# Attention scores and a recurrent gate as alternating 64-row products in place of stacked 128-row products

## The chip, the core and the metric

The kernel runs on one core of one Trainium2 chip. The metric is the device time of one execution in microseconds (us); smaller is better. The core has a matrix engine (TensorE, in the profile PE, and PEld for its loading of weights), VectorE (DVE), ScalarE (ACT), GpSimd (POOL) and SyncE (SP), which issues the transfers.

## What is computed

One decoder layer on 512 tokens of 1024 features. The parts that the change touches, cut from the reference:

```
qa = rms_norm(qa...); ka = rms_norm(ka...)                 # 8 heads of 64 features
s = einsum('bnqkgd,bnskd->bnkgqs', qb, kb) * HEAD_DIM**-0.5    # sliding window: own and previous block of 128 keys
...
s_own = einsum('bqhd,bshd->bqhs', q_c, k_c) * scale + own_bias # second attention (MoBA): 8 heads of 64 features
...
r = sigmoid(einsum('bsnc,ncd->bsnd', xb, ga_w) + ga_b)     # recurrence: 16 blocks of 64 features, two gates each
i = sigmoid(einsum('bsnc,ncd->bsnd', xb, gx_w) + gx_b)
```

Everything else (the input projection, the value products, the merge, the output projection, the gated MLP) is the same in both kernels.

## The kernel before

Features lie on the 128 partitions and tokens along the free axis. Every float32 operand of a product is split into a high part h with the 12 leading bits and a low part l (`split`), both in the type that TensorE takes at one column per cycle; a product x·y is made of the three passes h·h, h·l and l·h (`mm3`).

Scores and gates have a contraction of 64 features, half of the array's 128 rows. The kernel before fills the other half by stacking. A head of q (`turn_task`, key "q") has its high part on its own 64 partitions and its low part on the other 64; a head of k (key "k") has its high part on both halves of one tile and its low part on both halves of another, with two transfers per head that copy one half to the other. Then two passes of 128 rows make one head: stacked q against high k gives qh·kh + ql·kh, stacked q against low k gives qh·kl + ql·kl. `head_task` issues for each of the four query blocks of a head such a pair, over the keys that this block sees: 256, 256, 256 and 128 columns in a sliding-window head (kind "swa"), 512, 384, 256 and 128 in the other attention (kind "moba"). `lru_task` does the same for a recurrent gate: two blocks of 64 features, each stacked (high on one half, low on the other), two passes of 512 columns for each block, 8 times.

What follows a head's scores: VectorE adds the bias and takes the maximum (`E.ttr`), ScalarE takes exponentials, the matrix is transposed on TensorE (`E.tr`), split and multiplied with the values.

The order of the instructions is not written by hand. Every operation goes through the class `Emitter`, which records it; `flush` then simulates the engines with rough costs and lets each engine take the first operation whose operands are there. TensorE's long rows of work are the projections (`project`, and the loops over `qk` and `vc`), in the order of the table `ORDER`; the steps of attention and recurrence are generators that yield what they need (`Need`: tiles, PSUM banks, buffers) and are taken up between the products of the projections (`pump`). `FLY` says how many heads are in flight.

Of the kernel before, what the change touches and what calls it, by code (L numbers as in the profile page):

```python
# [25 lines left out]
# Columns of the per-feature vectors ("vec" input): feature f of a vector sits at partition f % 128,  # L26
# column f // 128 of its range.
# [8 lines left out]
# Columns of the shape-only constants ("cst" input).  # L36
# [24 lines left out]
class Buf:  # L61
    """A tile that is used again and again; Tile orders its uses, the emitter picks the ones that are free."""
# [21 lines left out]
class Emitter:  # L84
    """Emits instructions engine by engine and keeps a rough clock of each engine, so that the tensor engine's
    stream takes up work of the side tasks when its operands are there. The order it picks is one of many right
    ones: Tile puts in every wait."""
# [92 lines left out]
    # instructions  # L180
    def mm(self, out, lhsT, rhs, start, stop):
# [3 lines left out]
        else:  # L185
            cost = 4 * max(n, 128) / 2400 if n > 2 else 0.02
        self._go("pe", cost, [out], [lhsT, rhs], lambda: self.nc.tensor.matmul(out, lhsT, rhs, start=start, stop=stop),  # L187
                 rows=lhsT.shape[0] / 128)

# [78 lines left out]
    # the order of issue  # L268
    def flush(self):
        """Issue what was recorded: every engine takes, of its next few instructions, the first whose operands are  # L270
        there, by the same rough clock. Instructions that touch the same buffer keep their order."""
# [26 lines left out]
        def pe_cost(t, i):  # L298
            """The tensor engine runs at half its clock in a window that follows one with little work."""
# [54 lines left out]
    def cast(self, out, in_):  # L354
        """Copy (rounding to out's type) on whichever of the two engines would be done first."""
# [7 lines left out]
    def scale(self, out, in_, col):  # L363
        """out = in_ * col on whichever of the two engines would be done first."""
# [7 lines left out]
    def split(self, hi, lo, x):  # L372
        """hi + lo = x exactly, hi with the 12 leading bits."""
# [7 lines left out]
    def mm3(self, out, wh, wl, xh, xl, first, last):  # L381
        """out (+)= w.T x in three passes; what is left out is the product of the two low parts, below 2^-24."""
# [4 lines left out]
    # side tasks  # L387
# [34 lines left out]
    def pump(self, limit=LIMIT, force=False):  # L422
        """Take up steps of the side tasks that are ready, the oldest first, up to about limit us of tensor work."""
# [45 lines left out]
def hybrid_trunk_kernel(ctx: ExitStack, tc: tile.TileContext, xT, vec, cvec, cst, chot, rel, wm, w8, wz, wgate, wbr,  # L469
# [88 lines left out]
    def rsqrt(out, ssq, n, inv):  # L558
        """out = (ssq * inv + eps) ** -0.5: a first guess from the exponent, then three Newton steps."""
# [10 lines left out]
    def token_ssq(bk, sq, c0, nb, first=True, last=True):  # L570
        """Sums of squares over the features, a token per partition, a block of tokens per column."""
# [4 lines left out]
    def rsqrt_sqrt(out, st, ssq, n):  # L576
        """out = (ssq / D + eps) ** -0.5 from its rough square root st, by one Newton step."""
# [40 lines left out]
    # c on every partition; the sums of squares of x, a token per partition, beside it  # L618
# [12 lines left out]
    def warm(n):  # L631
        """Work for the tensor engine while it waits, so that its clock is up when the projections start."""
# [141 lines left out]
    def norm_task(bs, out, copy=False, v_first=None):  # L774
        """The banks bs with 8 heads each -> out, normalised but for the gain."""
# [27 lines left out]
    def turn_task(tn, srcs, gain, env, key):  # L803
        """Four blocks [token, feature] of two heads -> [feature, token], times the gain, split. A head of q has its
        high part on one half of the partitions and its low part on the other; a head of k has each part on both."""
        yield Need(tasks=(tn,))
        src = srcs()
        yield Need(aps=[x for x in src], banks=1, rslots=4 if key == "k" else 2)
# [3 lines left out]
        if key == "q":  # L812
            env["q"] = [E.rslot(), E.rslot()]
        else:
            env["kh"], env["kl"] = [E.rslot(), E.rslot()], [E.rslot(), E.rslot()]
        for u in range(2):
            p, o = half(u), half(1 - u)
            g, z = gain[p], bk.ap[p]
            if key == "q":
# [3 lines left out]
            else:  # L823
# [11 lines left out]
    def take_v(env, src, its):  # L835
        """src [token, (block, u, d)] of the token blocks its -> per block and head the high and the low parts."""
# [17 lines left out]
    def head_task(kind, tasks, qenv, kenv, venv, u, hd, oenv):  # L854
# [3 lines left out]
        if swa:  # L858
            loc = {3: (0, 0, 256), 2: (0, 256, 256), 1: (1, 0, 256), 0: (1, 256, 128)}
            keys = {i: max(i - 1, 0) * 128 for i in range(4)}  # L860
            ploc = {0: (0, 0, (0, 1)), 1: (0, 256, (1, 2)), 2: (1, 0, (2, 3)), 3: (1, 256, (3,))}
        else:
            loc = {3: (0, 0, 512), 2: (1, 0, 384), 0: (1, 384, 128), 1: (2, 0, 256)}
            keys = {i: 0 for i in range(4)}
            ploc = {0: (0, 0, (0, 1, 2, 3)), 1: (1, 0, (1, 2, 3)), 3: (1, 384, (3,)), 2: (2, 0, (2, 3))}
        wid = 256 if swa else 512
        sink = v("sinks", hd) if swa else -3.0e38
        yield Need(tasks=tasks, slots=nb + 1)
        T = E.slot()
        bias_tile(T.ap[:, :wid], d_swa if swa else d_moba, hd, wid)  # L870
        yield Need(aps=(qenv["q"][u].ap, kenv["kh"][u].ap, kenv["kl"][u].ap, T.ap), banks=nb,
                   slots=nb)
        bks = [E.bank() for _ in range(nb)]
        pr = [E.slot() for _ in range(nb)]
        mx, ngm, sm, ri = small(4), small(4), small(4), small(4)
        q, kh, kl = qenv["q"][u].r, kenv["kh"][u].r, kenv["kl"][u].r
        for i in (3, 2, 1, 0):
            b, c, n = loc[i]
            qs, ks = slice(i * 128, i * 128 + 128), slice(keys[i], keys[i] + n)
            E.mm(bks[b].ap[:, c:c + n], q[:, qs], kh[:, ks], True, False)  # L880
            E.mm(bks[b].ap[:, c:c + n], q[:, qs], kl[:, ks], False, True)
        for i in (3, 2, 1, 0):
            b, c, n = loc[i]
            E.ttr(pr[b].ap[:, c:c + n], bks[b].ap[:, c:c + n], T.ap[:, :n][:, ::-1], sink, OP.add,
                  OP.max, mx[:, i:i + 1])
# [609 lines left out]
```

## Time and profile before

| | |
|---|---|
| time, median of 3 runs | 907.24 us (906.32 to 908.49) |
| profiled execution, first to last instruction (span) | 904.7 us |
| PE busy | 895.8 us (99%) |
| PEld busy | 772.0 us (85%) |
| DVE busy | 630.1 us (70%) |
| ACT busy | 475.3 us (53%) |
| instructions of PE | 4730 |
| granted TensorE clock, mean | 0.998 |

The profile has no other time for the profiled execution than its span; the median of the runs is 2.5 us above it, which is what lies around the span. The page's busy share of PE is a union of pipelined instructions, so it only says that TensorE has nearly always a product under way. How long a product holds up the next one is read from the start of one row of the timeline to the start of the next, not from its own length: a product of 512 columns is listed with 0.39 us, and the next one starts 0.23 us after it. The timeline joins instructions of one group: "x8" stands for eight, with the shape of the first.

### The profile page before, as it was taken

How to read it: one execution, taken by the hardware profiler on the slowest of the kernel's cores; microseconds unless marked ns; L12 is line 12 of the kernel's file. 1: busy time of each engine (PE TensorE's matmuls, PEld its weight loads, DVE VectorE, ACT ScalarE, POOL GpSimd, SP SyncE). 2: the span in 40 equal slices, each digit the busy share in tenths (PEclk: the TensorE clock that was granted, in tenths of full speed). 3: DMA queues.
4: the chain of work that ended last, by engine and by line, in shares of the span. 5: the costliest groups of instructions: out<-in, count | busy, mean ns of one | idle time of the engine just before them, and what ended most of it. 6: DMA issues, size and time to landing. Idle time of an engine off the chain costs nothing.

```text
span 904.7 us, 12494 instructions
## 1 busy us (share of the span) xinstructions
PE 895.8 (99%) x4730; PEld 772.0 (85%) x4730; DVE 630.1 (70%) x1138; ACT 475.3 (53%) x763; POOL 1.8 (0%) x15
## 2 busy tenths in 40 slices
PE   7999999999999999999999999999999999999998
PEld 6889989889888888878888999888888888888888
DVE  6989989997876875887676888766656665522321
ACT  5366767985875898732223566544444444321110
POOL 0000000000000000000000000000000000000000
PEclk9999999999999999999999999999999999999999
DMA  8933532442254244586667655333222223333320
GB/s 315 347 119 99 155 99 93 129 163 95 73 172 155 90 140 152 184 275 214 229 226 285 213 173 172 123 101 107 97 93 93 93 97 103 104 116 105 117 82 24
DMA packets 44286, 131.70 MB, mean 146 GB/s; under 512 B 5393, under 2 KB 6937, under 8 KB 44226
## 3 DMA queue, kind: packets, MB, share of 16 engines
q1 hardware_dynamic: 44226, 130.90, 43.2%
q8 instruction: 37, 0.61, 0.3%
q14 instruction: 23, 0.19, 0.1%
HBM read 122.46 MB, written 5.80 MB: 142 GB/s over the span
## 4 chain that ended last, share of the span: by engine, by line
PE 93%; ACT 3%; DVE 2%; issue 1%; DMA 0%; SPq 0%; POOLq 0%; POOL 0%; ACTq 0%
PE bank L187 91%; PE bank L191 2%; ACT pair L213 2%; ACT L213 1%; DMA pair<-in_xT_dram 0%; DVE pair L243 0%; DVE pair L240 0%; DVE pair L246 0%; DVE lo L240 0%; ACT hi L213 0%; ACT rslot L213 0%; DVE rslot L240 0%; DVE pair L258 0%; SPq L264 0%; DVE rslot L243 0%
## 5 line engine op out<-in xcount | busy, mean ns | idle before, releaser
L187 PE MATMUL bank<-rslot,hi 128*128 128x512 f32 (+1 forms) x2332 | 656.8, 367 | 0.4 <-ACT rslot L213 0.4
L187 PEld LDWEIGHTS bank<-rslot,hi 128*128 128x128 f32 x2332 | 419.7, 189 | 70.1 <-ACT rslot L213 0.8
L187 PE MATMUL bank<-rslot,lo 128*128 128x512 f32 (+1 forms) x1166 | 427.0, 367 | 0.0
L240 DVE TENSOR_TENSOR lo<-raw,hi 128x1024 fp32r<-128x1024 f32 (+1 forms) x169 | 197.7, 1171 | 151.7 <-ACT hi L213 150.3
L213 ACT ACTIVATE hi<-raw 128x1024 fp32r<-128x1024 f32 (+1 forms) x153 | 156.6, 1025 | 185.3 <-PE bank L187 164.1
L187 PEld LDWEIGHTS bank<-rslot,lo 128*128 128x128 f32 x1166 | 219.9, 189 | 35.8
L187 PE MATMUL bank<-hi,rslot 128*128 128x256 f32 (+1 forms) x448 | 92.0, 315 | 0.1
L243 DVE SCALAR_TENSOR_TENSOR pair<-bank,V,pair 128x511 f32<-128x511 f32 (+2 forms) x112 | 83.6, 746 | 2.8 <-ACT pair L213 1.1
L187 PEld LDWEIGHTS bank<-hi,rslot 128*128 128x128 f32 x448 | 74.3, 190 | 6.3 <-issue 0.9
L213 ACT ACTIVATE rslot<-pair 128x512 fp32r<-128x512 f32 (+2 forms) x60 | 37.2, 622 | 76.7 <-DVE pair L240 72.6
L246 DVE CUSTOM_DVE_ANT_0 pair<-pair,pair,V 128x1024 f32<-128x1024 f32 x48 | 61.1, 1280 | 11.5 <-DMA pair<-in_wm_dram 11.5
L213 ACT ACTIVATE pair<-bank,V 128x512 f32<-128x512 f32 (+1 forms) x84 | 61.5, 732 | 4.8 <-PE bank L187 4.1
L213 ACT ACTIVATE pair<-bank 128x512 f32<-128x512 f32 (+2 forms) x75 | 43.2, 611 | 39.2 <-PE bank L187 38.6
L187 PE MATMUL bank<-lo,rslot 128*128 128x256 f32 (+1 forms) x224 | 62.5, 315 | 0.0
L213 ACT ACTIVATE pair<-pair 128x512 f32<-128x512 f32 (+1 forms) x62 | 35.2, 572 | 47.1 <-DVE pair L243 45.2
L240 DVE TENSOR_TENSOR rslot<-pair,rslot 128x512 fp32r<-128x512 f32 (+2 forms) x67 | 45.5, 680 | 15.2 <-ACT rslot L213 14.7
L240 DVE TENSOR_TENSOR pair<-pair,pair 128x512 f32<-128x512 f32 (+1 forms) x72 | 45.6, 636 | 12.6 <-ACT pair L213 7.6
L213 ACT ACT_TABLE_LOAD x37 | 47.5, 1283 | 5.2 <-PE bank L187 3.8
L187 PE MATMUL bank<-rslot,rslot 128*128 128x256 f32 (+3 forms) x288 | 48.8, 309 | 0.0
L187 PEld LDWEIGHTS bank<-rslot,rslot 128*128 128x128 f32 x288 | 43.4, 189 | 4.7 <-DVE rslot L240 0.8
L213 ACT ACTIVATE pair<-pair,small 128x256 f32<-128x256 f32 (+3 forms) x78 | 40.4, 529 | 11.3 <-DVE small L234 10.3
L187 PEld LDWEIGHTS bank<-lo,rslot 128*128 128x128 f32 x224 | 42.7, 190 | 2.6
(76 smaller groups left out, 412.5 us busy)
## 6 DMA issues: line engine op xcount, KB each, us to landing
raw<-in_wz_dram SPq DMA_DIRECT2D x50, 512.0 KB, 3.8
raw<-in_wup_dram SPq DMA_DIRECT2D x49, 512.0 KB, 3.3
pair<-in_wm_dram SPq DMA_DIRECT2D x48, 512.0 KB, 5.5
raw<-in_wdn_dram SPq DMA_DIRECT2D x22, 512.0 KB, 3.3
raw<-in_wout_dram SPq DMA_DIRECT2D x16, 512.0 KB, 3.3
pair<-in_xT_dram SPq DMA_DIRECT2D x16, 256.0 KB, 5.4
raw<-in_w_dram SPq DMA_DIRECT2D x8, 512.0 KB, 5.5
raw<-in_wbr_dram SPq DMA_DIRECT2D x16, 256.0 KB, 3.0
```

The source lines that it names most:

```text
L187: self._go("pe", cost, [out], [lhsT, rhs], lambda: self.nc.tensor.matmul(out, lhsT, rhs, start=start, stop=stop), rows=lhsT.shape[0] / 128)
L191: self._go("pe", 0.107, [out], [in_, ident], lambda: self.nc.tensor.transpose(out, in_, ident))
L213: self._go("act", c, outs, ins, lambda: self.nc.scalar.activation(out, in_, func, scale=scale, **kw), "tanh" if func == AF.Tanh else t)
L240: self._dve([out], [a, b], lambda: self.nc.vector.tensor_tensor(out, a, b, op=op))
L243: self._dve([out], [a, s, b], lambda: self.nc.vector.scalar_tensor_tensor(out, a, s, b, op0=op0, op1=op1))
L246: self._dve([out, accum], [a, b, s], lambda: self.nc.vector.tensor_tensor_reduce(out, a, b, 1.0, s, op0, op1, accum_out=accum))
```

## The change

`mm_group`, a new function of `Emitter`, records a list of products as one operation, whose products stay together on TensorE. The two heads of a pair, or the two blocks of a gate, now stay where they lie: one on partitions 0 to 63, the other on 64 to 127. Each product has 64 rows, with the program's tile size [64, 128] at row 0 or row 64 in place of [128, 128]. A group makes the three passes h·h, h·l, l·h, and in each pass first the product of head 0, then that of head 1, into two PSUM banks. `turn_task` makes one high and one low tile of all 128 partitions with one instruction of ScalarE and one of VectorE; the transfers that copied halves of k are gone. `head_task` is cut in two: `pair_task` does the scores of two heads, bank by bank, then spawns a `head_task` for each from the exponentials on. `FLY` counts pairs now (4 heads before, 2 pairs now). `lru_task` splits its 128 partitions at once.

```
-FLY, FIRST = 4, 5
+FLY, FIRST = 2, 5
...
+    def mm_group(self, mms):
+        def emit():
+            for o, w, x, a, b in mms:
+                self.nc.tensor.matmul(o, w, x, start=a, stop=b)
+        self._go("pe", sum(self.n(m[2]) / 4800 + 0.0025 for m in mms), ...
...
     turn_task:
-        for u in range(2):
-            p, o = half(u), half(1 - u)
-            g, z = gain[p], bk.ap[p]
-            if key == "q":
-                h = env["q"][u]
-                E.act(h.r[p], z, AF.Identity, scale=g)
-                E.stt(h.r[o], z, g, h.ap[p], OP.mult, OP.subtract)
-            else:
-                h, l = env["kh"][u], env["kl"][u]
-                E.act(h.r[p], z, AF.Identity, scale=g)
-                E.stt(l.r[p], z, g, h.ap[p], OP.mult, OP.subtract)
-                E.dma(h.ap[o], h.ap[p], 128)
-                E.dma(l.ap[o], l.ap[p], 128)
+        h, l = env[key] = [E.rslot(), E.rslot()]
+        E.act(h.r, bk.ap, AF.Identity, scale=gain)
+        E.stt(l.r, bk.ap, gain, h.ap, OP.mult, OP.subtract)
...
+    def pair_task(kind, tasks, qenv, kenv, venv, hds, oenv):
...
+        for b in range(nb):
+            yield Need(aps=(qh.ap, ql.ap, kh.ap, kl.ap, T[0].ap, T[1].ap), banks=2, slots=2)
+            bks = [E.bank(), E.bank()]
...
+            for i in its:
+                _, c, n = loc[i]
+                qs, ks = slice(i * 128, i * 128 + 128), slice(keys[i], keys[i] + n)
+                for x, y in ((qh, kh), (qh, kl), (ql, kh)):
+                    for u in range(2):
+                        mms.append((bks[u].ap[:, c:c + n], x.r[half(u), qs], y.r[half(u), ks], ...))
+            E.mm_group(mms)
...
     head_task:
-            E.mm(bks[b].ap[:, c:c + n], q[:, qs], kh[:, ks], True, False)
-            E.mm(bks[b].ap[:, c:c + n], q[:, qs], kl[:, ks], False, True)
...
     lru_task:
-        for u in range(2):
-            E.cast(xs[u].r[half(u)], xc.ap[half(u)])
-            E.tt(xs[u].r[half(1 - u)], xc.ap[half(u)], xs[u].ap[half(u)], OP.subtract)
...
-            E.mm(bks[u].ap, blk(h.r, o), xs[u].r, True, False)
-            E.mm(bks[u].ap, blk(l.r, o), xs[u].r, False, True)
+        E.split(xh, xl, xc.ap)
...
+        E.mm_group([(bks[u].ap, blk(w.r, (j % 2) * 2 + u)[half(u)], x.r[half(u)], w is h and x is xh, w is l)
+                    for w, x in ((h, xh), (h, xl), (l, xh)) for u in range(2)])
```

How the built program's order moves. On TensorE, the scores of one sliding-window head before stand so between products of a projection (a row is: source line, operation, PSUM bank <- moving operand, weights, and partitions x columns; `rslot` are the split q and k, `hi` and `lo` the projection's weights):

```order
L187 MATMUL bank7_142<-hi2_148,rslot15_90 128x256
L187 MATMUL bank6_141<-rslot19_94,rslot29_104 128x256
L187 MATMUL bank6_141<-rslot21_96,rslot29_104 128x256
L187 MATMUL bank6_141<-rslot19_94,rslot29_104 128x256
L187 MATMUL bank6_141<-rslot21_96,rslot29_104 128x256
L187 MATMUL bank0_135<-rslot19_94,rslot29_104 128x256
L187 MATMUL bank0_135<-rslot21_96,rslot29_104 128x256
L187 MATMUL bank0_135<-rslot19_94,rslot29_104 128x128
L187 MATMUL bank0_135<-rslot21_96,rslot29_104 128x128
L187 MATMUL bank1_136<-hi0_146,rslot0_75 128x256
```

And on TensorE at the first sliding-window scores of the changed kernel (two heads, in banks 3 and 5; `rslot18` and `19` are high and low k, `rslot24` and `25` high and low q):

```order
L187 MATMUL bank7_142<-hi2_148,rslot4_79 128x256
L194 MATMUL bank3_138<-rslot18_93,rslot24_99 128x256
L194 MATMUL bank5_140<-rslot18_93,rslot24_99 128x256
L194 MATMUL bank3_138<-rslot19_94,rslot24_99 128x256
L194 MATMUL bank5_140<-rslot19_94,rslot24_99 128x256
L194 MATMUL bank3_138<-rslot18_93,rslot25_100 128x256
L194 MATMUL bank5_140<-rslot18_93,rslot25_100 128x256
```

The products of one head, eight in a row, became groups of six for two heads and one query block, alternating between two banks and the two halves of the rows. Six more such products follow here before the projection goes on.

The two blocks of a recurrent gate on TensorE, before (`rslot52` and `54` are the two stacked inputs, moving; `rslot58` and `59` the high and low parts of the gates' weights):

```order
L187 MATMUL bank7_142<-rslot52_127,rslot58_133 128x512
L187 MATMUL bank7_142<-rslot52_127,rslot59_134 128x512
L187 MATMUL bank1_136<-rslot54_129,rslot58_133 128x512
L187 MATMUL bank1_136<-rslot54_129,rslot59_134 128x512
```

And a gate on TensorE in the changed kernel, with the products on either side of it (`rslot54` and `56` are the high and low input of both blocks, `rslot40` and `42` the weights):

```order
L187 MATMUL bank1_136<-rslot50_125,rslot17_92 128x128
L187 MATMUL bank1_136<-rslot51_126,rslot17_92 128x128
L194 MATMUL bank0_135<-rslot54_129,rslot40_115 128x512
L194 MATMUL bank2_137<-rslot54_129,rslot40_115 128x512
L194 MATMUL bank0_135<-rslot56_131,rslot40_115 128x512
L194 MATMUL bank2_137<-rslot56_131,rslot40_115 128x512
L194 MATMUL bank0_135<-rslot54_129,rslot42_117 128x512
L194 MATMUL bank2_137<-rslot54_129,rslot42_117 128x512
L187 MATMUL bank5_140<-hi1_147,rslot4_79 128x256
```

Four stacked products became six of 64 rows, between products of 128 rows. In the whole program 160 stacked products became 240 of 64 rows, which stand in 23 unbroken stretches of 6 to 24.

## Rows read from the trace of the kernel before

**Rows 1.** The page: span, busy share of PE, granted clock, chain that ended last.

```profile
span 904.7 us, 12494 instructions
...
PE 895.8 (99%) x4730; PEld 772.0 (85%) x4730; DVE 630.1 (70%) x1138; ACT 475.3 (53%) x763; POOL 1.8 (0%) x15
...
PEclk9999999999999999999999999999999999999999
...
PE 93%; ACT 3%; DVE 2%; issue 1%; DMA 0%; SPq 0%; POOLq 0%; POOL 0%; ACTq 0%
```

**Rows 2.** Busy us (and instructions) of each engine in four stretches of the span.

```profile
core 0: us, PE busy (x) PEld busy (x) DVE busy (x) ACT busy (x) POOL busy (x), PEclk, DMA share, GB/s
0.00:85.00 85.00, 79.61 (x437) 68.41 (x438) 73.61 (x162) 48.02 (x88) 0.96 (x7) 0.98 0.62 216
85.00:375.00 290.00, 290.00 (x1612) 252.40 (x1611) 239.82 (x545) 225.56 (x416) 0.69 (x7) 1.00 0.41 131
```

**Rows 3.** Waits of TensorE from 85 to 375 us: total, times, longest.

```profile
PEld bank L187 <- DVE rslot L240: 0.8, 3, 0.4
...
PEld bank L191 <- DVE rslot L240: 0.3, 1, 0.3
```

**Rows 4.** Timeline of PE: start us, listed us, group; three bursts and what follows.

```profile
90.57 1.06 PE L187 MATMUL bank<-rslot,rslot 128*128 128x256 f32 x8
91.46 0.33 PE L187 MATMUL bank<-hi,rslot 128*128 128x256 f32 x1
91.63 0.28 PE L187 MATMUL bank<-lo,rslot 128*128 128x256 f32 x1
...
172.61 1.38 PE L187 MATMUL bank<-rslot,rslot 128*128 128x512 f32 x8
173.83 0.29 PE L191 MATMUL bank<-CS,pair 128*128 128x128 f32 x1
...
239.66 1.07 PE L187 MATMUL bank<-rslot,rslot 128*128 128x512 f32 x4
240.57 0.39 PE L187 MATMUL bank<-rslot,hi 128*128 128x512 f32 x1
```

**Rows 5.** Timeline of PE around its one product of 32 rows.

```profile
66.12 0.28 PE L187 MATMUL bank<-lo,rslot 128*128 128x256 f32 x1
66.24 0.28 PE L187 MATMUL bank<-hi,rslot 128*128 128x256 f32 x1
66.45 1.03 PE L187 MATMUL bank<-pair,relt 32*16 32x512 f32 x2
67.41 0.39 PE L187 MATMUL bank<-hi,rslot 128*128 128x256 f32 x1
67.63 0.28 PE L187 MATMUL bank<-lo,rslot 128*128 128x256 f32 x1
```

**Rows 6.** Timeline of the weight loads (PEld) in the same place.

```profile
66.12 0.19 PEld L187 LDWEIGHTS bank<-hi,rslot 128*128 128x128 f32 x1
66.45 0.11 PEld L187 LDWEIGHTS bank<-pair,relt 32*16 32x16 f32 x2
67.41 0.19 PEld L187 LDWEIGHTS bank<-hi,rslot 128*128 128x128 f32 x1 [0.85 <-issue]
67.52 0.19 PEld L187 LDWEIGHTS bank<-lo,rslot 128*128 128x128 f32 x1
```

**Rows 7.** Timeline of PE around a full-height product of the other float type.

```profile
520.70 0.28 PE L187 MATMUL bank<-rslot,lo 128*128 128x256 f32 x1
520.82 0.59 PE L187 MATMUL bank<-pair,ones 128*128 128x256 f32 x2
521.06 0.59 PE L187 MATMUL bank<-rslot,hi 128*128 128x256 f32 x2
521.49 0.28 PE L187 MATMUL bank<-rslot,lo 128*128 128x256 f32 x1
```

**Rows 8.** Groups of PEld by shape: busy us, mean ns of one, idle before.

```profile
L187 PEld LDWEIGHTS bank<-rslot,rslot 128*128 128x128 f32 x288 | 43.4, 189 | 4.7 <-DVE rslot L240 0.8
L187 PEld LDWEIGHTS bank<-pair,relt 32*16 32x16 f32 x2 | 0.1, 90 | 0.1
```

**Rows 9.** Groups of ACT by shape: q and k split, input of the gates split.

```profile
L213 ACT ACTIVATE rslot<-bank,gq 64x512 fp32r<-64x512 f32 x16 | 10.9, 683 | 0.8 <-PE bank L191 0.5
L213 ACT ACTIVATE rslot<-pair 64x512 fp32r<-64x512 f32 x12 | 7.5, 628 | 4.1 <-DVE pair L243 3.9
L213 ACT ACTIVATE rslot<-bank,V 64x512 fp32r<-64x512 f32 x10 | 6.8, 682 | 0.8 <-PE bank L191 0.6
```

**Rows 10.** Groups of DVE by shape, the same work.

```profile
L243 DVE SCALAR_TENSOR_TENSOR rslot<-bank,gq,rslot 64x512 fp32r<-64x512 f32 x16 | 12.0, 750 | 0.4
L240 DVE TENSOR_TENSOR rslot<-pair,rslot 64x512 fp32r<-64x512 f32 x16 | 11.0, 686 | 0.5
```

**Rows 11.** The tile rslot: the transfers of k's halves (issue ns), their time to landing.

```profile
L264 SPq DMA_DIRECT2D rslot<-rslot x20: 461/529/553, 77.2 to 234.0; - x20
...
DMA to landing us min/median/max: 2.2/2.2/3.1
```

More of the change, by code (lines that the diff above doesn't have):

```diff
@@ L188, in mm @@
                  rows=lhsT.shape[0] / 128)
+    def mm_group(self, mms):
+        def emit():
+            for o, w, x, a, b in mms:
+                self.nc.tensor.matmul(o, w, x, start=a, stop=b)
+        self._go("pe", sum(self.n(m[2]) / 4800 + 0.0025 for m in mms), list({m[0].tensor.name: m[0] for m in mms}.values()),
+                 [x for m in mms for x in m[1:3]], emit)
     def tr(self, out, in_, ident):
@@ L807, in turn_task @@
         src = srcs()
-        yield Need(aps=[x for x in src], banks=1, rslots=4 if key == "k" else 2)
+        yield Need(aps=[x for x in src], banks=1, rslots=2)
         bk = E.bank()
@@ L849, in v_of @@
         return env["v"][kb // 2].r[:, o:o + 128]
-    def head_task(kind, tasks, qenv, kenv, venv, u, hd, oenv):
+    def pair_task(kind, tasks, qenv, kenv, venv, hds, oenv):
+        swa = kind == "swa"
+        if swa:
+            loc = {3: (0, 0, 256), 2: (0, 256, 256), 1: (1, 0, 256), 0: (1, 256, 128)}
+            keys = {i: max(i - 1, 0) * 128 for i in range(4)}
+        else:
+            loc = {3: (0, 0, 512), 2: (1, 0, 384), 0: (1, 384, 128), 1: (2, 0, 256)}
+            keys = {i: 0 for i in range(4)}
+        nb = 2 if swa else 3
+        wid = 256 if swa else 512
+        yield Need(tasks=tasks, slots=4)
+        T = [E.slot(), E.slot()]
+        for u in range(2):
+            bias_tile(T[u].ap[:, :wid], d_swa if swa else d_moba, hds[u], wid)
+        qh, ql = qenv["q"]
+        kh, kl = kenv["k"]
+        pr = [[], []]
+        mx = [small(4), small(4)]
+        ngm = [small(4), small(4)]
+        for b in range(nb):
+            yield Need(aps=(qh.ap, ql.ap, kh.ap, kl.ap, T[0].ap, T[1].ap), banks=2, slots=2)
+            bks = [E.bank(), E.bank()]
+            for u in range(2):
+                pr[u].append(E.slot())
+            its = [i for i in (3, 2, 1, 0) if loc[i][0] == b]
+            mms = []
+            for i in its:
+                _, c, n = loc[i]
+                qs, ks = slice(i * 128, i * 128 + 128), slice(keys[i], keys[i] + n)
+                for x, y in ((qh, kh), (qh, kl), (ql, kh)):
+                    for u in range(2):
+                        mms.append((bks[u].ap[:, c:c + n], x.r[half(u), qs], y.r[half(u), ks], x is qh and y is kh,
+                                    x is ql))
+            E.mm_group(mms)
+            for u in range(2):
+                sink = v("sinks", hds[u]) if swa else -3.0e38
+                for i in its:
+                    _, c, n = loc[i]
+                    E.ttr(pr[u][b].ap[:, c:c + n], bks[u].ap[:, c:c + n], T[u].ap[:, :n][:, ::-1], sink, OP.add,
+                          OP.max, mx[u][:, i:i + 1])
+            E.drop(*bks)
+        E.drop(*T)
+        for u in range(2):
+            E.ts(ngm[u], mx[u], -1.0, None, OP.mult)
+            drop_small(mx[u])
+        ts = [E.spawn(head_task(kind, pr[u], ngm[u], venv, u, hds[u], oenv, loc, keys)) for u in range(2)]
+        yield Need(tasks=ts)
+        oenv["h"], oenv["l"] = E.rslot(), E.rslot()
+        E.split(oenv["h"], oenv["l"], oenv["o"].ap)
+        E.drop(oenv["o"])
+        E.drop(*qenv["q"])
+        if not swa:
+            E.drop(*kenv["k"], *venv["v"])
@@ L855, in head_task @@
+    def head_task(kind, pr, ngm, venv, u, hd, oenv, loc, keys):
         swa = kind == "swa"
@@ L858, in head_task @@
         if swa:
-            loc = {3: (0, 0, 256), 2: (0, 256, 256), 1: (1, 0, 256), 0: (1, 256, 128)}
-            keys = {i: max(i - 1, 0) * 128 for i in range(4)}
             ploc = {0: (0, 0, (0, 1)), 1: (0, 256, (1, 2)), 2: (1, 0, (2, 3)), 3: (1, 256, (3,))}
         else:
-            loc = {3: (0, 0, 512), 2: (1, 0, 384), 0: (1, 384, 128), 1: (2, 0, 256)}
-            keys = {i: 0 for i in range(4)}
             ploc = {0: (0, 0, (0, 1, 2, 3)), 1: (1, 0, (1, 2, 3)), 3: (1, 384, (3,)), 2: (2, 0, (2, 3))}
[L866 to L879, printed above, removed]
-            E.mm(bks[b].ap[:, c:c + n], q[:, qs], kh[:, ks], True, False)
-            E.mm(bks[b].ap[:, c:c + n], q[:, qs], kl[:, ks], False, True)
[L882 to L885, printed above, removed]
-        E.drop(T, *bks)
-        E.ts(ngm, mx, -1.0, None, OP.mult)
+        sm, ri = small(4), small(4)
         yield Need(aps=[ngm], table="exp")
@@ L892, in head_task @@
         if swa:
-            E.act(ri, ngm, AF.Exp, bias=sink)
+            E.act(ri, ngm, AF.Exp, bias=v("sinks", hd))
         yield Need(aps=[sm])
@@ L932, in head_task @@
         E.act(t.ap[0:64, :], bk.ap[64:128, :], AF.Copy)
-        yield Need(aps=[t.ap], slots=1, rslots=2)
+        yield Need(aps=[t.ap], slots=1)
         if "o" not in oenv:
@@ L937, in head_task @@
         E.drop(bk, t)
-        oenv["n"] = oenv.get("n", 0) + 1
-        if oenv["n"] == 2:
-            oenv["h"], oenv["l"] = E.rslot(), E.rslot()
-            E.split(oenv["h"], oenv["l"], oenv["o"].ap)
-            E.drop(oenv["o"])
-            E.drop(*qenv["q"])
-            if not swa:
-                E.drop(*kenv["kh"], *kenv["kl"], *venv["v"])
     OA = [{} for _ in range(4)]
@@ L1073, in lru_task @@
         yield Need(aps=(xc.ap,), rslots=2)
[L1075 to L1079 removed]
+        xh, xl = E.rslot(), E.rslot()
+        E.split(xh, xl, xc.ap)
+        yield Need(aps=(xh.ap, xl.ap), banks=2, slots=2, tasks=(tg,), table="sigmoid")
         h, l = gw[j // 2]
         bks = [E.bank(), E.bank()]
[L1082 to L1086 removed]
+        E.mm_group([(bks[u].ap, blk(w.r, (j % 2) * 2 + u)[half(u)], x.r[half(u)], w is h and x is xh, w is l)
+                    for w, x in ((h, xh), (h, xl), (l, xh)) for u in range(2)])
+        E.drop(xh, xl)
         gw[j // 2, "n"] = gw.get((j // 2, "n"), 0) + 1
```

25 lines of the change are left out of this document (7 added, 18 removed).

## The prediction

> **What bounds the kernel now.** The page comes first: PE has a product under way for 99% of a span of 904.7 us, the chain that ended last is 93% PE, and the granted clock stands in the highest tenth in every slice [rows 1]. So the time is the sum of what TensorE's instructions hold up, and only what changes that sum counts. The table of stretches says where: every score and every gate lies in the stretch 85 to 375 us, in which PE is busy for 290.00 of 290.00 us, with DVE at 239.82 and ACT at 225.56 [rows 2]. The waits of that stretch are 0.8 and 0.3 us [rows 3]. Nothing there waits for the work that feeds the scores; what gets cheaper on other engines is hidden, and what gets longer or shorter on TensorE goes into the end time one for one.
>
> What a product holds up is read from start to start. Four gate products of 512 columns take 240.57 - 239.66 = 0.91 us, 0.227 each. A sliding-window head (six of 256 columns, two of 128) takes 91.46 - 90.57 = 0.89 us, and the product behind it 91.63 - 91.46 = 0.17 [rows 4], where products of 256 columns follow each other at 0.12 (66.24 - 66.12) [rows 5]. So 0.94 us in all, 0.72 for the six and 0.11 for each of the small two. That 0.11 is not columns (128 are half of 256): it is the weight load. When TensorE resumes after a pause one load starts at 67.41 and the next at 67.52 [rows 6]: a load holds up the next load for 0.11 us, and hides only behind a product that is longer. A MoBA head takes 173.83 - 172.61 = 1.22 [rows 4] and, with 0.05 behind it as there, 1.27; less two of 512 (0.45), two of 256 (0.24) and two of 128 (0.22) that leaves 0.18 for each of 384.
>
> **What it removes.** Before: 8 x 0.94 = 7.5 us (sliding window), 8 x 1.27 = 10.2 us (MoBA), 8 gates x 0.91 = 7.3 us: 25.0 us of the 290 are the products in question.
>
> **What takes their place, if the two halves stream together.** Three passes, and in each the two heads side by side, cost three times one head's list: sliding window 3 x (3 x 0.12 + 0.11) = 1.41 for a pair, x 4 = 5.6; MoBA 3 x (0.227 + 0.18 + 0.12 + 0.11) = 1.91, x 4 = 7.6; gates 3 x 0.227 = 0.68, x 8 = 5.4. Sum 18.7, a gain of 6.3 us. No row shows two products of 64 rows side by side, so this is one end. The other end is that they go one after the other: six products for each four, 25.0 x 1.5 = 37.5 us, a loss of 12.5.
>
> Between them is a third value. Each pass now has two weight loads. If loads still follow each other at 0.11 us [rows 6], whatever half they go to, a pass of two cannot be shorter than 0.22. Then sliding window is 12 x 0.22 = 2.64 for a pair (10.6), MoBA 3 x (0.227 + 3 x 0.22) = 2.66 (10.6), gates 5.4: 26.6 us, a loss of 1.7. I take the parallel value: loads and products of different halves read different partitions, and nothing in the rows is a resource that both need; but rows 6 show loads of one tile only, so this stays open. The Trainium skill, "TensorEngine Tiling (Array Packing)", section Tiling Modes, says that different tiles can execute LdWeights and Matmul in parallel. No run here shows it yet; by it the sum is the 18.7 above, and without it 26.6.
>
> **Going to half rows and back.** There is one place in the trace where TensorE leaves the full array: a product with tile size [32, 32], in two float passes [rows 5]. Before it the last full product starts at 66.24 and would be through at 66.36; the weights for the small one are not loaded until 66.45 [rows 6], though loads elsewhere start together with the product before. Behind it the two passes (66.45 and 66.89, by their even share of the 0.44 that 512 columns cost in four-pass float: twice 0.227) are through at 67.33 or so, and the next load starts at 67.41, put down to "issue", which is no wait that the profile knows [rows 6]. The full product that should stand at 67.33 + 0.12 is followed only at 67.63. Sum: from 66.24 to 67.63 are 1.39 us, the work in it is 0.12 + 0.88 + 0.12 = 1.12; 0.27 us are lost, by the row. It isn't the float type: a full-height product of the same kind stands in the stream with nothing lost (521.49 - 520.82 = 0.67, which is 2 x 0.215 + 2 x 0.12) [rows 7]. The load in that place had 16 columns (90 ns); one of 128 has 189 ns [rows 8], 0.10 us more that nothing hides. So 0.37 us for a visit to the half-row array. The low end is 0 (a visit to 64 x 128 is not a visit to 32 x 32, and could be free), the high end 0.48, if the second half's load (0.11) is exposed too. I take 0.37, since the only row of such a visit gives it. With 23 stretches of 64-row products: 8.5 us (0 to 11.0).
>
> The same page of the Trainium skill, section Tiling Modes, states the rule that speaks against this change: changing the tiling mode, not just the tile, drains the TensorE. Rows 5 and 6 agree, with 0.27 us for one visit; without the rule the sum would be a gain of 6.3 us.
>
> **Other edits, costed at nothing.** Splitting q and k on 128 partitions at once halves 26 instructions of ACT and of DVE (13 x 0.68 and 13 x 0.75 us), the gate inputs' split halves 12 of ACT and 16 of DVE (6 x 0.63 and 8 x 0.69) [rows 9, 10]; the 20 transfers that landed 2.2 us after their issue are gone [rows 11]. All of it lies beside the full PE stretch [rows 2]. A group is one operation now, and its first product waits for both heads' q and k, both bias tiles and two banks; behind it on PE stand the projections. The nearest rows are the waits of today, 1.1 us in all [rows 3]: that is what could go, and I allow as much to come. Two pairs in flight are the four heads of before.
>
> **Sum.** 18.7 + 8.5 - 25.0 = +2.2 us on a profiled span of 904.7, 906.9; with the 2.5 us that lie between span and median, 907.24 + 2.2 = 909.4. Own range of this case, with a visit at 0.27 to 0.48 us (6.2 to 11.0) and the 1.1 us of waits either way: 906 to 913.
>
> **The rivals.**
> - *The visits are cheap* (0 to 0.27 us). For it: 64 x 128 keeps all columns, and the one row is of a tile that cut both. Against it: a load that is held back until the array is empty would be held back by any change of tile. 907.24 - 6.3 = 900.9 with none of it, 907.1 with 0.27; middle 904.
> - *The weight loads queue* (slower). Its place is every pass of 384 columns or fewer, its price 0.22 for a pass of two; it decides as soon as a product lasts less than two loads, which is all but 512 columns. For it: the 0.11 between loads [rows 6] and the small products that it already bounds [rows 4]. Against it: the halves share no partition. +1.7 + 8.5 = 917.4; 908.9 if the visits are free.
> - *The halves do not stream together*: the change doesn't do what it says. For it: no row shows two products at once. 907.24 + 12.5 + 8.5 = 928; 919.7 with free visits.
>
> **How the numbers follow.** Chances: the forecast 0.40, cheap visits 0.26, queued loads 0.22, no streaming together 0.12. A measurement of this kernel tells 0.2% (1.8 us) from no change, so faster is below 905.4 and slower above 909.1. Of cheap visits 0.20 lies below 905.4 and 0.06 within; of the forecast 0.16 lies within and 0.24 above; of queued loads 0.02 and 0.20; the last case is all above. Faster 0.20, same 0.24, slower 0.56. The range leaves out the last case and the far ends of the two before it: 901.5 to 919.
>
> **What would show it.** In the timeline of PE after the change, a gate's six products from first start to the next full product's start: 0.68 us and about 0.37 for the visit is the forecast; 0.68 with no gap ahead of the first and behind the last is cheap visits; starts 0.227 apart one by one are no streaming together. A sliding-window group of 256 columns decides on loads: pairs at 0.12 or at 0.22 us. The gap ahead of the group should show weight loads that start only after the last full product, marked issue. DVE and ACT should be down by some 15 and 13 us, with no gain from it. Wrong would be: 64-row stretches with the full rate and no pause, or new waits of PE for DVE or ACT of several us from 85 to 375 us.

## The result and the profile after

The changed kernel takes 913.57 us (median of 4 runs, 911.16 to 914.62) where the kernel before takes 907.23 on the same chip: 1.0077 times as long, with a 95% interval of 1.0061 to 1.0093. That is 6.3 us slower, three times the 2.2 us of the forecast, in the same direction, inside the stated range of 901.5 to 919 us and 0.6 us above the forecast's own range, which ended at 913.

The page of the profile after, in the lines that answer to [rows 1]: more PE work and a longer span, less work on DVE and ACT. The run that was profiled took 914.32 us.

```profile
span 912.5 us, 12544 instructions
...
PE 900.8 (99%) x4810; PEld 768.3 (84%) x4810; DVE 614.9 (67%) x1119; ACT 451.9 (50%) x735; POOL 1.7 (0%) x15
...
PE 96%; DVE 2%; ACT 1%; DMA 0%; issue 0%; SPq 0%; DVEq 0%
```

DVE lost 15.2 us and ACT 23.4 us of work (15 and 13 were foreseen; five loads of ScalarE's function tables fewer, 32 in place of 37, make another 6.4), and nothing was gained by it, since PE is still the chain. Busy time by stretch, as in [rows 2]:

```profile
0.00:85.00 85.00, 79.53 (x429) 68.41 (x429) 72.66 (x164) 44.52 (x83) 0.96 (x7) 0.96 0.68 233
85.00:375.00 290.00, 287.75 (x1669) 242.60 (x1668) 223.83 (x521) 200.82 (x386) 0.69 (x7) 0.99 0.37 115
```

In the stretch that had no idle PE before (290.00 of 290.00) PE now idles for 2.25 us. Three things are to be read from the timeline: what a stretch of 64-row products costs, where the idle time is, and what the clock does behind it.

**A gate and a score stretch.** PE around one gate and around the first sliding-window scores (start, listed length, group). In the changed kernel L194 is `mm_group`, so these are the 64-row products, and L187 is every other product:

```profile
294.88 0.39 PE L187 MATMUL bank<-rslot,hi 128*128 128x512 f32 x1
295.20 0.97 PE L194 MATMUL bank<-rslot,rslot 64*128 64x512 f32 x6
296.10 0.50 PE L187 MATMUL bank<-rslot,hi 128*128 128x512 f32 x1
296.44 0.40 PE L187 MATMUL bank<-rslot,lo 128*128 128x512 f32 x1
...
85.60 0.40 PE L187 MATMUL bank<-hi,rslot 128*128 128x256 f32 x2
85.92 0.98 PE L194 MATMUL bank<-rslot,rslot 64*128 64x256 f32 x12
86.83 0.39 PE L187 MATMUL bank<-lo,rslot 128*128 128x256 f32 x1
87.06 0.40 PE L187 MATMUL bank<-hi,rslot 128*128 128x256 f32 x2
```

The gate: from the last full product (294.88) to the second one behind (296.44) are 1.56 us; less two products of 0.227 that leaves 1.10. Six products of 512 columns in 1.10 us cannot be one after the other (1.36): they are three passes of two, 0.68, and 0.42 for the visit. The scores: 87.06 - 85.60 = 1.46, less three products of 0.12, is 1.10; six passes of two are 0.72, and 0.38 is the visit. Against [rows 4], where the gate took 0.91, a gate is 0.2 us longer.

The weight loads of the same two places:

```profile
295.20 0.53 PEld L194 LDWEIGHTS bank<-rslot,rslot 64*128 64x128 f32 x6 [0.35 <-issue]
296.10 0.19 PEld L187 LDWEIGHTS bank<-rslot,hi 128*128 128x128 f32 x1 [0.37 <-issue]
296.21 0.19 PEld L187 LDWEIGHTS bank<-rslot,lo 128*128 128x128 f32 x1
...
85.48 0.31 PEld L187 LDWEIGHTS bank<-hi,rslot 128*128 128x128 f32 x2
85.92 0.77 PEld L194 LDWEIGHTS bank<-rslot,rslot 64*128 64x128 f32 x12
86.83 0.19 PEld L187 LDWEIGHTS bank<-lo,rslot 128*128 128x128 f32 x1
```

No load starts beside the product ahead of a switch. Around the gate the first load of each kind stands behind a pause that the profile puts down to "issue", on entry and on exit, as it did behind the one small product of the kernel before [rows 6]; around the scores the loads pause for 0.13 us on entry (85.79 to 85.92) and 0.14 on exit, which the profile doesn't mark. Summed in this way over all 23 stretches, scores and gates hold TensorE for 27.8 us, of which the passes of two (at the rates of the full array) are 18.6 and the visits 9.2: 0.40 us each. Before it was 25.0, by the bursts of [rows 4] times the number of heads and gates.

**The new wait.** Waits of TensorE from 85 to 375 us, the longest ones (total, times, longest), to be held against [rows 3]; and PE's timeline at the place:

```profile
PEld bank L194 <- issue: 4.5, 13, 0.4
PEld bank L187 <- issue: 4.0, 11, 0.4
PEld bank L199 <- DVE pair L242: 2.9, 2, 2.4
PE bank L199 <- DVE pair L242: 2.2, 2, 2.0
```

```profile
182.55 0.39 PE L187 MATMUL bank<-rslot,lo 128*128 128x512 f32 x1
184.91 1.31 PE L199 MATMUL bank<-CS,pair 128*128 128x128 f32 x10 [1.97 <-DVE pair L242]
186.50 2.40 PE L199 MATMUL bank<-CS,pair 128*128 128x128 f32 x10 [0.28 <-DVE pair L242]
```

The issue waits are the visits. The third and fourth rows are something else: transposes of a softmax (L199) stand in the order ahead of the projections, and VectorE is not through with scaling it (L242 multiplies by a column). PE idles for 2.0 us and once more for 0.3. What VectorE does in that time, ahead of and in the scaling:

```profile
182.44 1.23 DVE L266 TENSOR_TENSOR_SCAN pair<-pair,pair 128x512 f32<-128x512 f32 x1
183.59 0.15 DVE L263 RECIPROCAL small<-small 128x4 f32<-128x4 f32 x1
183.77 1.28 DVE L242 TENSOR_SCALAR pair<-pair,small 128x512 f32<-128x512 f32 x4
```

A scan of 1.23 us stands ahead of the reciprocal and the scaling that the transposes need; VectorE itself has no pause there.

**The clock behind it.** Stretches around that wait (the column before the last two is the granted clock, a share of 2.4 GHz):

```profile
182.00:187.00 5.00, 2.75 (x18) 2.02 (x17) 4.69 (x15) 4.96 (x18) 0.00 (x0) 0.94 0.35 107
187.00:190.00 3.00, 3.00 (x14) 2.73 (x13) 3.00 (x9) 3.00 (x8) 0.00 (x0) 0.53 0.27 81
```

From 186.4 to 189.8 us the clock is at its lower level, 1.2 GHz, behind a stretch in which PE was busy for 2.75 of 5 us. At 0.53 of full speed 1.4 us of work is lost in the second row, and at 0.94 another 0.3 in the first: 1.7 us.

It is not so in every run. The kernel of the second experiment below (three passes of one half, then three of the other) has the same wait in its trace, 1.93 us from 180.88 on, and its clock stays up behind it:

```profile
180.00:185.00 5.00, 2.79 (x19) 2.05 (x18) 4.69 (x15) 4.96 (x18) 0.00 (x0) 1.00 0.34 107
185.00:188.00 3.00, 2.65 (x21) 2.26 (x20) 3.00 (x9) 3.00 (x8) 0.00 (x0) 1.00 0.48 150
```

That run took 911.34 us. The four runs of the changed kernel have mean granted clocks of 0.994, 1.000, 0.998 and 0.994, and times of 914.32, 911.16, 912.81 and 914.62 in that order. The mean doesn't say where the clock was low: from 10 to 20 us, at the start, it is 0.83 in the trace before, 0.66 in the one after and 1.00 in this third one. The kernel before has no such wait, and in the runs beside the later experiments its time goes with the mean clock too, from 904.5 us at 1.000 to 908.4 at 0.996. At a mean clock of 1.000 the two kernels are still 6.5 us apart, so the loss does not need the half clock; the visits and the wait make 5.0 of that, and the rest is not traced.

The profiled run's span is 7.8 us longer than the span before. By products that both kernels have, 1.1 us of it lies ahead of all changed products: the product of 32 rows, at 66.45 before [rows 5], now stands here,

```profile
67.57 1.03 PE L187 MATMUL bank<-pair,relt 32*16 32x512 f32 x2
```

with the lower clock at the start beside it. Another 5.4 us lie between there and the first product of 256 columns behind the long projections (491.15 before, 497.67 after), and 1.0 us between there and 560 us, where a wait of 0.6 us for ACT is new; 0.3 us stand behind the last product. The middle part holds 2.8 us from the scores and gates (27.8 - 25.0), 2.2 us of wait and 1.7 us of half clock. That is 1.3 us more than it lost; what was gained back there is not traced to rows (a wait of 0.4 us for ACT at 387 us, of the trace before, is gone).

### The profile page after: what moved, and what is told of

Read it like the earlier page. It is cut to its first block, busy times and chain, and to the rows that moved or that the text cites. A ratio compares the mean times of both kernels' runs of the same rounds, so it can differ in the third digit from the quotient of the medians.

```text
span 912.5 us, 12544 instructions
## 1 busy us (share of the span) xinstructions
PE 900.8 (99%) x4810; PEld 768.3 (84%) x4810; DVE 614.9 (67%) x1119; ACT 451.9 (50%) x735; POOL 1.7 (0%) x15
## 4 chain that ended last, share of the span: by engine, by line
PE 96%; DVE 2%; ACT 1%; DMA 0%; issue 0%; SPq 0%; DVEq 0%
PE bank L187 92%; PE bank L194 2%; PE bank L199 2%; DMA pair<-in_xT_dram 0%; DVE pair L254 0%; ACT pair L221 0%; DVE pair L242 0%; DVE pair L248 0%; DVE pair L266 0%; DVE lo L248 0%; SPq L272 0%; DVE rslot L251 0%; ACT hi L221 0%; ACT rslot L221 0%; DVE pair L251 0%
## 5 line engine op out<-in xcount | busy, mean ns | idle before, releaser
L187 PE MATMUL bank<-rslot,hi 128*128 128x512 f32 (+1 forms) x2332 | 658.9, 368 | 0.6 <-ACT hi L221 0.6
L187 PEld LDWEIGHTS bank<-rslot,hi 128*128 128x128 f32 x2332 | 419.8, 189 | 73.3 <-issue 2.6
L187 PE MATMUL bank<-rslot,lo 128*128 128x512 f32 (+1 forms) x1166 | 426.9, 367 | 0.0
L248 DVE TENSOR_TENSOR lo<-raw,hi 128x1024 fp32r<-128x1024 f32 (+1 forms) x169 | 197.4, 1170 | 157.3 <-ACT hi L221 156.2
L187 PEld LDWEIGHTS bank<-rslot,lo 128*128 128x128 f32 x1166 | 219.7, 189 | 36.1 <-issue 0.4
L187 PE MATMUL bank<-hi,rslot 128*128 128x256 f32 (+1 forms) x448 | 92.5, 316 | 0.0
L187 PEld LDWEIGHTS bank<-hi,rslot 128*128 128x128 f32 x448 | 74.5, 190 | 6.8 <-issue 1.6
L221 ACT ACTIVATE rslot<-pair 128x512 fp32r<-128x512 f32 (+1 forms) x56 | 34.5, 622 | 79.2 <-DVE pair L248 69.0
L187 PE MATMUL bank<-lo,rslot 128*128 128x256 f32 (+1 forms) x224 | 62.7, 315 | 0.0
L248 DVE TENSOR_TENSOR pair<-pair,pair 128x512 f32<-128x512 f32 (+1 forms) x76 | 48.4, 638 | 15.3 <-ACT pair L221 10.3
L248 DVE TENSOR_TENSOR rslot<-pair,rslot 128x512 fp32r<-128x512 f32 (+1 forms) x59 | 39.7, 678 | 19.1 <-ACT rslot L221 19.1
L187 PEld LDWEIGHTS bank<-lo,rslot 128*128 128x128 f32 x224 | 42.7, 190 | 2.7
L221 ACT ACTIVATE pair<-pair,small 128x256 f32<-128x256 f32 (+3 forms) x74 | 37.8, 522 | 1.5 <-DVE small L263 0.7
L221 ACT ACTIVATE rslot<-bank 128x512 fp32r<-128x512 f32 (+3 forms) x64 | 24.0, 444 | 14.8 <-PE bank L187 10.6
L251 DVE SCALAR_TENSOR_TENSOR pair<-pair,bank 128x512 f32<-128x512 f32 (+1 forms) x25 | 16.5, 662 | 20.1 <-PE bank L187 20.0
```

What stands on the lines that cost most here:

```text
L221: self._go("act", c, outs, ins, lambda: self.nc.scalar.activation(out, in_, func, scale=scale, **kw), "tanh" if func == AF.Tanh else t)
L248: self._dve([out], [a, b], lambda: self.nc.vector.tensor_tensor(out, a, b, op=op))
L251: self._dve([out], [a, s, b], lambda: self.nc.vector.scalar_tensor_tensor(out, a, s, b, op0=op0, op1=op1))
```

## The experiments

**The price of a visit by itself, and whether two halves stream together.** Three kernels put two extra products of 512 columns behind each of 39 up-projections of the gated MLP, where PE has no pause in the trace before. What they compute is read by nobody.

```
 (the kernel before)
             project(z.ap, wh, wl, slice(0, S), Fh, Fl)
+d_full      E.mm_group([(x.ap, blk(wh, 0), Fh[0].r, True, True) for x in (x1, x2)])
+d_half      E.mm_group([(x.ap, blk(wh, 0)[half(u)], Fh[0].r[half(u)], True, True) for u, x in enumerate((x1, x2))])
+d_same      E.mm_group([(x.ap, blk(wh, 0)[half(0)], Fh[0].r[half(0)], True, True) for x in (x1, x2)])
```

> The kernel before, with two more products of 128 rows and 512 columns behind each of the last 39 up-projections of the gated MLP, into two banks that nobody reads. The control for the next two. Every theory: 78 x 0.227 = 17.7 us more, 925 us, no gap around them in the timeline.

> The same place and count, but the two products have 64 rows each, one at row 0 and one at row 64. Theory (a visit to the half-row array costs 0.40 us, the two halves stream together): 39 x (0.227 + 0.40) = 24.5 us more, 932 us. Rival (visits are free, and what the changed kernel loses is its order): 39 x 0.227 = 8.9 us more, 916 us. Rival (halves one after the other): 39 x 0.454 = 17.7 us more and the visits on top, 925 to 941 us.

> As the run with the two halves, but both products use row 0. Theory: they cannot stream together, 39 x (0.454 + 0.40) = 33.3 us more, 941 us, 8.9 us above the run with two halves. Rival (the two halves do not stream together either): the same time as that run.

Measured: 925.13, 931.74 and 940.52 us, with the kernel before at 906.49 (ratios 1.0206, 1.0279 and 1.0376, each within 0.003). All three lie within 0.6 us of the times that the theory gave. From kernel to kernel, the halves cost 6.6 us more than the full array (6.8 by the theory) and the same half 8.8 us more than the halves (8.9): 0.225 us for each of the 39 places, one pass of 512 columns. One stretch of the two halves, then one of the same half, in PE's timeline:

```profile
701.62 0.39 PE L187 MATMUL bank<-rslot,lo 128*128 128x512 f32 x1
701.94 0.50 PE L194 MATMUL bank<-rslot,hi 64*128 64x512 f32 x2
702.38 0.73 PE L187 MATMUL bank<-rslot,hi 128*128 128x512 f32 x2
702.94 0.40 PE L187 MATMUL bank<-rslot,lo 128*128 128x512 f32 x1
```

```profile
699.83 0.39 PE L187 MATMUL bank<-rslot,lo 128*128 128x512 f32 x1
700.15 0.73 PE L194 MATMUL bank<-rslot,hi 64*128 64x512 f32 x2
700.81 0.73 PE L187 MATMUL bank<-rslot,hi 128*128 128x512 f32 x2
701.38 0.39 PE L187 MATMUL bank<-rslot,lo 128*128 128x512 f32 x1
```

702.94 - 701.62 less three products of 0.227 is 0.64: one pass of 0.227 and a visit of 0.41. 701.38 - 699.83 less the same is 0.87: two passes and the same visit. Visits that are free, and halves that go one after the other, both fall. Two products on two halves cost more (0.64) than two products on the full array (0.45).

**Whether the alternation matters.** The changed kernel, with three passes of one half and then three of the other:

```
-                for x, y in ((qh, kh), (qh, kl), (ql, kh)):
-                    for u in range(2):
+                for u in range(2):
+                    for x, y in ((qh, kh), (qh, kl), (ql, kh)):
...
-... for w, x in ((h, xh), (h, xl), (l, xh)) for u in range(2)])
+... for u in range(2) for w, x in ((h, xh), (h, xl), (l, xh))])
```

> The changed kernel with each group in another order: three passes of half 0, then three of half 1, in place of alternating. Theory (products start in the program's order, so only the last of a triple runs beside the first of the next): a group of six lasts five passes in place of three, longer stretches 17 in place of 12; 18.6 us of passes become 27 to 31, so 922 to 926 us. Rival (TensorE pulls the other half's products ahead, the alternation buys nothing): 913.6 us.

Measured: 912.21 us, ratio to the kernel before 1.0068 (1.0038 to 1.0099). The theory misses by 10 us and the rival holds. A gate in its timeline:

```profile
142.13 0.28 PE L187 MATMUL bank<-lo,rslot 128*128 128x256 f32 x1
142.35 0.97 PE L194 MATMUL bank<-rslot,rslot 64*128 64x512 f32 x6
143.25 0.51 PE L187 MATMUL bank<-hi,rslot 128*128 128x256 f32 x2
143.59 0.28 PE L187 MATMUL bank<-lo,rslot 128*128 128x256 f32 x1
```

143.59 - 142.13 less three products of 0.12 is 1.10 us, to the hundredth the alternating gate of above. In the program two products of half 0 stand between the first of that half and the first of half 1; by their starts the products still come in pairs, 0.01 us apart (0.003 where they alternate), so the two halves run side by side all the same.

**Each half of the change alone.** Gates alone (the new `lru_task` in the kernel before), and attention alone (the old `lru_task` in the changed kernel):

```
 p_gate: the kernel before, with
-            E.mm(bks[u].ap, blk(h.r, o), xs[u].r, True, False)
-            E.mm(bks[u].ap, blk(l.r, o), xs[u].r, False, True)
+        E.mm_group([(bks[u].ap, blk(w.r, (j % 2) * 2 + u)[half(u)], x.r[half(u)], ...
...
 p_attn: the changed kernel, with those lines the other way round
```

> Only the recurrent gates changed, attention as before. 8 visits. Theory (visits): 8 x (0.68 + 0.41 - 0.91) = +1.4 us, 908.7 us if the waits stay as in the kernel before. Rival (the loss is in attention's order alone and the gates gain): 8 x (0.68 - 0.91) = -1.8 us, 905.4 us.

> Only attention changed, gates as before. 15 visits of 0.38 us and 13.2 us of passes in place of 17.7: theory (visits, and a new wait that the order of issue makes by chance): +1.2 us and whatever waits its own order has, 908.5 to 913 us. Rival (pairs make two softmaxes fall due at once, so the wait of 2 us for VectorE and the half clock behind it belong to pairs): the wait is here too, 911 to 913 us.

Measured: gates alone 911.50 us (1.0057, 1.0042 to 1.0072), attention alone 913.02 us (1.0074, 1.0059 to 1.0089), the kernel before 906.56. In the traces the eight gates hold TensorE for 8.8 us (7.3 before), the scores for 18.8 us (17.7 before): +1.5 and +1.1 us, as the visits want. The times are 4.9 and 6.5 us longer. Of the 3.4 and 5.4 us that are left, idle PE from 85 to 375 us makes 2.2 and 3.9 us, in rows that differ:

```profile
85.00:375.00 290.00, 287.83 (x1612) 246.56 (x1611) 237.38 (x541) 215.90 (x402) 0.84 (x7) 1.00 0.43 136
```

```profile
85.00:375.00 290.00, 286.10 (x1646) 244.44 (x1642) 229.03 (x527) 209.31 (x398) 0.70 (x7) 0.99 0.37 120
```

The first row is gates alone, the second attention alone. Gates alone has no pair of heads, and it too got waits that the kernel before doesn't have: its longest is 1.1 us, for a split on VectorE. So for gates both theories miss the time; the size of the visits is right, the waits were not in it. Attention alone has the wait of the changed kernel again (2.2 us for DVE pair L242), with the clock at 0.50 from 183.6 to 186.9 us, and a second one of 2.2 us for a split on VectorE at 373 us. Both theories allowed the first.

**Whether the wait belongs to pairs or to an order.** The planner takes a scan on VectorE for half of the 1.23 us that the trace shows. Raising that, and the add with maximum a little, makes it plan another order of the same kernel (and move a few copies between ACT and DVE):

```
-        self._dve([out], [a, b], lambda: ...tensor_tensor_scan(out, a, b, init, OP.mult, OP.add))
+        self._dve([out], [a, b], lambda: ...tensor_tensor_scan(out, a, b, init, OP.mult, OP.add), extra=0.63)
...
-            out, a, b, 1.0, s, op0, op1, accum_out=accum))
+            out, a, b, 1.0, s, op0, op1, accum_out=accum), extra=0.03)
```

> The changed kernel, the planner's costs of two VectorE operations raised to what the trace shows (the scan 1.23 us, the add with maximum 0.03 us more); the instructions are the same, their order may move. Theory (the wait of 2 us at 183 us is an accident of an order planned with a VectorE that is too fast): the wait goes, the clock stays up, only visits are left: 909.5 to 911 us. Rival (the wait belongs to pairs): 912 to 914 us.

> Attention changed, gates as before, with the planner's VectorE costs raised: the twin of the run with attention alone, which measured 913.0 us with 5.3 us more waits than before. Theory (the wait belongs to the order that was planned, not to pairs): waits back near 3.4 us, 16 visits left, +1.3 us: 907 to 909 us. Rival (pairs make VectorE late whatever the order): 911 to 914 us.

> The kernel before with the same planner's costs: the control of the run with the changed kernel. Theory: its waits of 85 to 375 us are 1 us and stay so, 906.5 to 908 us. Rival (these costs help or hurt any order): over 909 or under 906.

Measured: the changed kernel so planned 909.47 us (1.0031, 1.0016 to 1.0046), attention alone so planned 908.52 us (1.0017, 1.0004 to 1.0029): 4.1 and 4.5 us less than their twins. The theory holds for both (to 0.1 us), and the rival for neither. Their PE in the stretch (the changed kernel, then attention alone):

```profile
85.00:375.00 290.00, 288.77 (x1675) 243.21 (x1674) 224.90 (x524) 205.73 (x393) 0.69 (x7) 1.00 0.38 124
```

```profile
85.00:375.00 290.00, 289.70 (x1670) 247.35 (x1669) 231.83 (x533) 213.50 (x404) 0.70 (x7) 1.00 0.38 122
```

Idle PE goes from 2.25 to 1.23 and from 3.90 to 0.30 us; the wait for DVE pair L242 is in neither, and in the changed kernel scores and gates still hold TensorE for 28.0 us, in 24 stretches now. So the wait is not a property of pairs. It isn't healed by better costs either: the kernel before, planned with the same costs, takes 926.53 us (1.0226, 1.0209 to 1.0243), far from its expectation. It has no pairs, and its transposes (L191) wait for VectorE too; at 507 us, behind attention, it has a wait that no earlier run had:

```profile
PE bank L187 <- ACT hi L213: 9.1, 1, 9.1
PE bank L191 <- DVE wide L240: 2.5, 1, 2.5
```

What this control shows is how much hangs on the order, with the few copies that move with it: 20 us, with no product changed.

Another order of the changed kernel, from a group's cost that is 0.2 us higher:

```
-        self._go("pe", sum(self.n(m[2]) / 4800 + 0.0025 for m in mms), ...
+        self._go("pe", 0.2 + sum(self.n(m[2]) / 4800 + 0.0065 for m in mms), ...
```

> The changed kernel with the planner's cost of a group raised by 0.2 us and to what single products cost. Theory (every new order draws its waits by chance, visits stay): 23 visits, 27.8 us for scores and gates in the trace, and 0 to 5 us of waits, 909 to 915 us. Rival (the wait of 2 us came from the group's cost being planned at half): no wait of TensorE over 0.5 us from 85 to 375 us, 909.5 us.

Measured: 910.29 us (1.0042, 1.0027 to 1.0058), 28.5 us for scores and gates, PE busy for 289.39 of the 290 us; its longest wait in the stretch is 0.9 us in the weight loads and 0.5 us in the products. That lies inside the theory's range and near the rival's figure too, so it doesn't say whether the group's cost was the reason; it does say that a second order of this kernel comes out near 910. The wait for DVE pair L242 is not in it.

**Fewer visits.** All scores of a pair as one group, over 4 or 6 banks, gates as before:

```
-        for b in range(nb):
-            yield Need(aps=(qh.ap, ql.ap, kh.ap, kl.ap, T[0].ap, T[1].ap), banks=2, slots=2)
-            bks = [E.bank(), E.bank()]
+        yield Need(aps=(qh.ap, ql.ap, kh.ap, kl.ap, T[0].ap, T[1].ap), banks=2 * nb, slots=2 * nb)
+        bks = [[E.bank() for _ in range(nb)] for u in range(2)]
...
+        E.mm_group(mms)      # the four query blocks of both heads
```

> Attention changed so that all scores of a pair are one group (4 or 6 banks at once): 8 visits in place of 15; gates as before. Theory (0.38 us per visit): scores cost 13.2 + 8 x 0.38 = 16.2 us in the trace where the kernel before has 17.6, a gain of 1.4 us if the order brings no wait: 905.2 us; with waits as attention alone had, 910.5. Rival (what a visit costs grows with its length): 17.5 us or more in the trace.

> The same with the planner's VectorE costs raised. Theory: scores cost 16.2 us in the trace, waits near those of the kernel before, 905 to 907 us, the one version that could be faster than the kernel before. Rival (holding six banks at once makes TensorE wait for VectorE): over 909 us, with waits for DVE in the trace.

Measured: 907.03 us (1.0000, 0.9988 to 1.0012), and with the raised costs 908.48 us (1.0018, 1.0005 to 1.0031). A whole sliding-window pair in the timeline of the first:

```profile
88.91 0.28 PE L187 MATMUL bank<-hi,rslot 128*128 128x256 f32 x1
89.12 1.62 PE L194 MATMUL bank<-rslot,rslot 64*128 64x256 f32 x24
90.67 0.38 PE L187 MATMUL bank<-hi,rslot 128*128 128x256 f32 x1
90.90 0.28 PE L187 MATMUL bank<-lo,rslot 128*128 128x256 f32 x1
```

90.90 - 88.91 less two products of 0.12 is 1.75: twelve passes of two at 1.41, and 0.34 for the visit, no more than for a stretch half as long. The scores hold TensorE for 16.1 us in both, 1.6 less than before, as the theory has it. But the order brought waits again (one of 2.4 us for DVE rslot L248 in the first, one of 1.5 us for ACT in the second), and the gain is gone: the first lies between the 905.2 and 910.5 us of its theory, the second above the 907 of its theory and below the 909 of the rival. No version was faster than the kernel before.

## Why the prediction came out as it did

**What bounds the kernel: right.** TensorE's stream is the end; 15 and 23 us less work on VectorE and ScalarE brought no gain.

**Passes of two, 18.7 us: right.** The halves stream together, shown by the two halves against the same half, 0.225 us apart. The 18.6 of the trace takes that rate over, and what is then left for a visit is the same in stretches of 6 and of 24 products. The choice that weight loads of two halves don't queue was right as well: if loads of the two halves queued at 0.11 us, the twelve products of 256 and the visit at 85.92 would have taken 1.32 + 0.38 and took 1.10. By this the trace agrees with what the Trainium skill ("TensorEngine Tiling (Array Packing)", Tiling Modes) says, that different tiles can load weights and multiply in parallel.

**A visit, 0.37 us: right in kind, slightly small.** It is 0.40 in the 23 stretches and 0.41 by itself. The row of one 32 x 32 product foretold it, including what the wider weight load adds. The same page of the Trainium skill states that a change of tiling mode drains TensorE, and the trace agrees for 64 x 128: no load or product starts beside the last one of the other kind.

**Sum of both: +2.2 forecast, +2.8 measured** in the trace.

**Waits: the term that was mis-sized.** It was put at up to 1.1 us either way, from the waits of the order of before [rows 3], on the ground that PE has other work to go on with. That step failed: an order in which a planner has left 1 us of waits doesn't tell what a new order will have. The trace has 2.2 us of new wait, and the profiled run 1.7 us of half clock behind it, together more than the change itself costs. Two other orders of the same change are without that wait and measure 2.9 and 3.7 us more than the kernel before beside them, where the forecast had 2.2. The half clock stands behind this wait in the traces of the changed kernel and of attention alone, and not in that of the kernel with three passes of each half, so it is part of some runs only. What decides that stays open, as does why the planned order was wrong by 2 us just there.

**The rivals.** Cheap visits and halves in sequence are refuted by the kernels with extra products, queued loads by the timeline. A new wait of PE for DVE was named among the signs of being wrong, but has no term in the sum and no rival of its own. That 913.57 us lies inside the range is luck: above 913 the range is there for queued loads, which did not happen.

## What to carry to other kernels

Two 64-row products side by side save streaming time, but each stretch of them costs 0.40 us here to enter and leave together; six passes of 256 columns or three of 512 do not earn that back (a gate saved 0.23 us per visit), and only longer unbroken stretches did (24 products: 16.1 us for all scores in place of 17.7). Where TensorE is the bound and a planner sets the order, an edit of a few us has to be judged on several orders, since another planned order moved these kernels by 1.5 to 20 us: look at the start-to-start sum of the products that were changed, and at the waits separately.

## What the runs showed of the hardware

- Products of the two row halves start 2 to 5 ns apart in nearly all pairs of the alternating groups, and so do their weight loads. A stretch with three of one half ahead of three of the other runs just as fast (1.10 us for a gate in either order), in pairs that start 10 ns apart, so TensorE does not hold the second half's products behind those of the first.
- A visit costs the same whether 2, 6, 12 or 24 products stand in it (0.33 to 0.43 us where the neighbours are plain products of a projection).
- The granted clock stood at 1.2 GHz from 186.4 to 189.8 us, behind a pause of 2.0 us in PE, in the profiled run of the changed kernel; in the trace of the kernel with three passes of each half a pause of 1.9 us at the same place left it at 2.4 GHz.
